# Hybrid decoder layer on one core: the order of short-convolution rows, the steps of the output projection's residuals, and the tile order of its last step

## The chip, the cores and the metric

One core of one Trainium2 chip. The metric is the device time of one execution in microseconds; the kernel before took 1410.79 us (median of 3 runs, 1409.48 to 1411.41).

## What is computed

One layer of a decoder step: 1104 rows of 1024 values (16 meta tokens, 1024 of a prompt, 64 of eight samples of eight). Cut to what matters here:

```python
hn = rmsnorm(h, norm_mix_pre)
proj = hn @ w_in                       # gate_b, gate_c, hv (512 each), z, xbc, dt
u = gate_c * hv
conv_u, _ = causal_dwconv(u, buf_sc, sconv_w)              # 3 taps
ya = group_rmsnorm(gate_b * conv_u, sconv_norm, 8)         # short convolution
...                                                        # SSD mixer gives yb (1024 wide)
mix = concatenate([ya, yb], -1) @ w_out
h = h + rmsnorm(mix, norm_mix_post)
f = rmsnorm(h, norm_ffn_pre)
y = h + rmsnorm((silu(f @ w_gate) * (f @ w_up)) @ w_down, norm_ffn_post)
```

All of it is float32; each product is made of matmuls of high and low parts (`hi`/`lo`, `...h`/`...l` in the names), two or three for one.

## The kernel before

The input is normalised and transposed (to 45 us), then projected row by row (a row is 128 channels for all tokens, in three pieces of 272, 320 and 512 columns, `CUTS`). Up to about 400 us PE (TensorE) does the SSD mixer's rows; the `z` rows and the short convolution's rows are the filling, which a generator hands out. The short convolution has four groups of 128 channels, j = 0 to 3, and three kinds of row for each, in the order of the string `SORD` (L43): `c` is the gate (`pc`, copied to `gc` by ACT), `v` the values (`ph`; DVE multiplies them by the gate, L649, and then the three taps follow, ACT L249 and DVE L252, written over `gc`), `b` the output (`pb`; L662 multiplies by `gc`, then squares, a matmul `sn` for the group sums, square root, reciprocal L672, product L673, and the store of the row to `d_ya`, L674, on SP's queue). The pieces of a row take turns in two PSUM buffers (`acc`, `NACC` = 2): the third piece waits until the first has been read.

Then the output projection, L985 to L1027: the token tiles go in three groups, (1,2,3), (4,9,5) and (6,7,8), with twelve steps n = 0 to 11 each, one for every 128 rows of `w_out` (k = 4 to 11, then 0 to 3). A step loads a piece of weights (`wo`), splits it (`woh` by ACT L998, `wol` by DVE L999) and does the matmuls L1007 of the group's tiles one after the other into two banks each. The mixing tiles come from DRAM (`mrb`, `mra`, L947) and are split into `mhb`/`mlb` and `mha`/`mla` (L954, L98). A finished group's tiles are copied (`h_tile`, L887 on ACT and L888 on DVE) and kept in `pend`. In the steps of the group after, `residual` is called for them at the steps of the list `RES`, and `fn_tile` at the steps of `FNS`. `residual` is a square sum on ACT (`ms`, L147), mean on DVE (L139), power on POOL (L141), and L899 and L900 on DVE; `fn_tile` another square sum (`hs`), power, L916 on DVE, eight transposes on PE (`fT`, L928) and copies to `xr` and `B1` (L931 or L933). For the last group both are called behind the loop, around `first(0)`, the first product of the FFN.

The FFN's gate and up products go by seven products for each block; `first(q)` (L1062) does four half products on PE: gate, up, gate, up (`xg`, `xu`; L1048). After a first half ACT copies it (`p1g`, `p1u`, L1077); the second half adds to the same PSUM, so it waits for that copy. The PSUM of `xg` is that of the last group's third tile in the list. Behind it come sums on DVE (L1189 to L1202: `T2`, `T3`, `T1`, `B22`; L1041: `s2g` and others) for the next products, `yg` and `zg`. The down projection ends the kernel.

The program's order is not the order on the engines: the scheduler of the framework takes an instruction by its priority and by a model of when it could start. `tc.high_priority(offset=...)` puts an instruction forward by so many places. So a change of a list can move rows on every engine.

## Time and profile before

| | us |
|---|---|
| median of 3 runs | 1410.79 |
| the profiled execution | 1407.59 |
| its span, first to last instruction | 1405.9 |
| PE busy | 1371.6 |
| DVE busy | 973.9 |
| ACT busy | 586.6 |
| mean granted clock of PE | 0.997 |

The profile is of one execution. A row of the timeline has its start, its length, engine, line, operation, output from inputs, shape, and in brackets how long the engine was idle before it and what ended that. DVE is VectorE, ACT ScalarE, POOL GpSimd, SP the queue that issues the DMAs. Where a release is named, it is the last one that the profile saw.

### The profile page before, as it was taken

The numbers are of one execution on the slowest core, as the hardware profiler recorded it, in microseconds if no ns is written. First come the engines' busy times: TensorE is split into PE (matmuls) and PEld (weight loads), VectorE is DVE, ScalarE is ACT, GpSimd is POOL, SyncE is SP. The second block draws the span as 40 slices with busy tenths as digits, with TensorE's granted clock in tenths as the row PEclk, the third lists the DMA queues.
The fourth block names the chain that finished last, engine by engine and source line by source line (L and its number), as shares of the span: only waits on it lengthen the run. The fifth ranks groups of instructions, "written<-read, shape, count | busy, mean of one in ns | idle before, by whom it ended". The sixth has DMA issues, their size and how long they took to land.

```text
span 1405.9 us, 22011 instructions
## 1 busy us (share of the span) xinstructions
PE 1371.6 (98%) x8841; PEld 1229.4 (87%) x8841; DVE 973.9 (69%) x1334; ACT 586.6 (42%) x947; POOL 50.0 (4%) x106
## 2 busy tenths in 40 slices
PE   7999999999999998999999999999999999999997
PEld 5889998878888986887889999999999998888886
DVE  6655457877888987687489877666767666455565
ACT  6465345434354344566554232222332234343431
POOL 1000000000000100011000000000000000000001
PEclk9999999999999999999999999999999999999999
DMA  6135347667736447765445553445333469655554
GB/s 213 47 103 153 94 125 197 204 175 204 216 116 209 130 133 273 249 225 179 149 137 181 183 203 115 161 165 175 133 131 113 163 222 323 226 178 168 168 166 139
DMA packets 212543, 240.51 MB, mean 171 GB/s; under 512 B 33421, under 2 KB 161505, under 8 KB 212442
## 3 DMA queue, kind: packets, MB, share of 16 engines
q1 hardware_dynamic: 212442, 239.12, 53.4%
q8 instruction: 69, 1.13, 0.3%
q14 instruction: 32, 0.26, 0.1%
HBM read 170.29 MB, written 68.79 MB: 170 GB/s over the span
## 4 chain that ended last, share of the span: by engine, by line
PE 84%; DVE 6%; DMA 5%; ACT 2%; issue 1%; SPq 1%; POOL 0%; DVEq 0%; POOLq 0%; ACTq 0%
PE d L1391 15%; PE px L220 10%; PE o L1007 9%; PE yg L1048 7%; PE yu L1048 7%; PE zg L1048 4%; PE zu L1048 4%; PE pz L220 4%; PE xg L1048 4%; PE xu L1048 4%; PE pc L220 3%; PE pb L220 3%; DMA M<-d_a 2%; PE ph L220 2%; PE pd L572 1%
## 5 line engine op out<-in xcount | busy, mean ns | idle before, releaser
L220 PE MATMUL px<-xh,whi 128*128 128x272 f32 (+2 forms) x288 | 94.8, 337 | 0.0
L220 PE MATMUL px<-xl,whi 128*128 128x272 f32 (+2 forms) x288 | 93.7, 333 | 0.0
L220 PE MATMUL px<-xh,wlo 128*128 128x272 f32 (+2 forms) x288 | 93.4, 332 | 0.0
L98 DVE TENSOR_TENSOR wlo<-raw,whi 128x1024 fp32r<-128x1024 f32 x32 | 39.1, 1220 | 44.8 <-ACT whi L106 43.5
L999 DVE SCALAR_TENSOR_TENSOR wol<-wo,vec,woh 128x1024 fp32r<-128x1024 f32 x36 | 46.0, 1278 | 31.5 <-ACT woh L998 31.5
L220 PE MATMUL pz<-xh,whi 128*128 128x256 f32 (+2 forms) x192 | 64.8, 337 | 0.2 <-DVE z L627 0.2
L220 PE MATMUL pz<-xh,wlo 128*128 128x256 f32 (+2 forms) x192 | 63.9, 333 | 0.0
L220 PE MATMUL pz<-xl,whi 128*128 128x256 f32 (+2 forms) x192 | 63.8, 332 | 0.0
L998 ACT ACTIVATE woh<-wo,vec 128x1024 fp32r<-128x1024 f32 x36 | 41.4, 1150 | 49.7 <-PE o L1007 44.1
L220 PEld LDWEIGHTS px<-xh,whi 128*128 128x128 f32 x288 | 54.5, 192 | 4.2
L220 PEld LDWEIGHTS px<-xl,whi 128*128 128x128 f32 x288 | 54.0, 190 | 4.2 <-issue 0.2
L220 PEld LDWEIGHTS px<-xh,wlo 128*128 128x128 f32 x288 | 54.0, 191 | 3.7
L1391 PE MATMUL d<-wd,B01h 128*128 128x512 f32 x176 | 54.2, 389 | 0.0
L252 DVE SCALAR_TENSOR_TENSOR xa<-xr,vec,xa 128x1128 f32<-128x1128 f32 x36 | 50.1, 1391 | 1.2 <-ACT xa L249 0.5
L1391 PE MATMUL d<-wd,T3h 128*128 128x512 f32 x152 | 46.8, 389 | 0.0
L1007 PE MATMUL o<-wol,mhb 128*128 128x512 f32 x144 | 44.3, 393 | 1.4 <-DVE wol L999 1.4
L1391 PE MATMUL d<-wd,B11h 128*128 128x512 f32 x144 | 44.2, 389 | 0.0
L1391 PE MATMUL d<-wd,T2h 128*128 128x512 f32 x144 | 44.2, 389 | 0.0
L556 ACT ACTIVATE M<-M,a_tok 128x128 f32<-128x128 f32 (+1 forms) x72 | 21.7, 383 | 47.8 <-DMA M<-d_a 37.9
L279 ACT ACTIVATE xr<-px 128x272 f32<-128x272 f32 (+2 forms) x36 | 16.3, 456 | 60.0 <-PE px L220 60.0
L1007 PE MATMUL o<-woh,mhb 128*128 128x512 f32 x144 | 39.5, 397 | 1.9 <-DVE gc L662 0.8
L1007 PE MATMUL o<-woh,mlb 128*128 128x512 f32 x128 | 40.0, 390 | 0.0
(691 smaller groups left out, 4094.5 us busy)
## 6 DMA issues: line engine op xcount, KB each, us to landing
wo<-in_w_out_dram SPq DMA_DIRECT2D x36, 512.0 KB, 3.5
raw<-in_w_in_dram SPq DMA_DIRECT2D x32, 512.0 KB, 6.0
wg<-in_w_gate_dram SPq DMA_DIRECT2D x11, 1024.0 KB, 8.4
wu<-in_w_up_dram SPq DMA_DIRECT2D x11, 1024.0 KB, 5.1
xr<-in_w_down_dram SPq DMA_DIRECT2D x11, 1024.0 KB, 5.3
d_t<-xr SPq DMA_DIRECT2D x11, 1024.0 KB
xt<-in_x_prompt_dram SPq DMA_DIRECT2D x16, 512.0 KB, 6.4
M<-d_a SPq DMA_DIRECT2D x16, 512.0 KB, 5.9
```

Source lines behind the costliest of these rows:

```text
L98: V.tensor_tensor(out=out, in0=a, in1=hi.bitcast(F32), op=ALU.subtract)
L220: PE.matmul(acc, (hi, lo, hi)[q][:, wk], (xh, xh, xl)[q][t][:, k, o:], start=n_ == 0, stop=n_ + 1 == len(order))
L252: V.scalar_tensor_tensor(out=dst, in0=part(row, i), scalar=wv[:, wcol(i):wcol(i) + 1], in1=dst, op0=ALU.mult, op1=ALU.add)
L279: S.activation(row[:, rc], pt[:, pc], AF.Copy)
L556: S.activation(M[:w, h, :w], M[:w, h, :w], AF.Relu, scale=-1.0, bias=a_s)
L572: PE.matmul(pdv[64 * e:64 * e + 64, h // 2, :w], xd[:w, h * 64:(h + 1) * 64], Ms[h // 8][:w, h % 8, :w], start=True, stop=True)
L998: S.activation(hi, raw, AF.Copy, scale=nv)
L999: V.scalar_tensor_tensor(out=lo, in0=raw, scalar=nv, in1=hi[:, :].bitcast(F32), op0=ALU.mult, op1=ALU.subtract)
L1007: PE.matmul(accs[i][c], l[:, kb, :], r_[:, c * 512:(c + 1) * 512], start=n == 0 and q == 0, stop=n == 11 and q == len(steps) - 1)
L1048: PE.matmul(acc[:, c, 0:W1], w_[l][k], b[r_][:, k, c * W1:(c + 1) * W1], start=start and k == 0 and x == 0, stop=k == 3 and x == 2, skip_g ...
L1391: PE.matmul(accs[t], sx[x][:, tl], wx[y], start=st and x + y == 0, stop=en and x == 1, skip_group_check=n not in OPENS)
```

## The change

Four edits. `SORD` has `v3` before `b2` instead of after it. `RES` and `FNS`, the steps at which a finished group's residuals and norm tiles are issued, go from 1, 2, 3 and 5, 6, 7 to 1, 3, 5 and 4, 6, 8. In the last group's last step the list of tiles is turned, so that tile 8's matmuls stand first, and since `pend` is made from the same list, its copies, residual and norm tile come first too (8, 6, 7). The copy by DVE instead of ACT in `fn_tile` goes from tile 8 to tile 7, which is now the last.

```diff
-SORD = "c0 c1 v0 v1 b0 c2 b1 v2 c3 b2 v3 b3"
-RES = [1, 2, 3]
-FNS = [5, 6, 7]
+SORD = "c0 c1 v0 v1 b0 c2 b1 v2 c3 v3 b2 b3"
+RES = [1, 3, 5]
+FNS = [4, 6, 8]
...
-                if q == 1 and i == GROUPS[-1][-1]:
+                if q == 1 and i == GROUPS[-1][1]:
                     V.tensor_copy(xr[q][n][:, :, cs], pt[:, :, ts])
...
+            if n == 11 and gi + 1 == len(GROUPS):
+                tiles = tiles[2:] + tiles[:2]
             for i in tiles:
```

Lines from L1001 on have numbers higher by 2 in the changed kernel.

DVE at the end of the short convolution, before. `gc_4220` is group 2's row and `gc_4618` group 3's, `pb` the pieces of a `b` row:

```order
425 L999 SCALAR_TENSOR_TENSOR wol_5202<-wo_5199,vec,woh_5201 128x1024
426 L673 TENSOR_TENSOR gc_4220<-gc_4220,sq_4849 128x512
427 L252 SCALAR_TENSOR_TENSOR gc_4618<-u_4921,vec,gc_4618 128x1024
428 L252 SCALAR_TENSOR_TENSOR gc_4618<-u_4921,vec,gc_4618 128x64
429 L588 TENSOR_TENSOR yf_5418<-yf_5418,zt_5420 128x1024
430 L252 SCALAR_TENSOR_TENSOR gc_4618<-u_4921,vec,gc_4618 128x1024
431 L252 SCALAR_TENSOR_TENSOR gc_4618<-u_4921,vec,gc_4618 128x64
432 L593 TENSOR_TENSOR zt_5420<-zt_5420 128x2x256
433 L662 TENSOR_TENSOR gc_4618<-pb_0_5022,gc_4618 128x256
434 L662 TENSOR_TENSOR gc_4618<-pb_1_5056,gc_4618 128x320
435 L98 TENSOR_TENSOR mlb_5180<-mrb_5177,mhb_5179 128x1024
```

The same place now, from the first read of group 3's `b` row on; its taps stand at 410 to 416, between the rows of group 2:

```order
424 L662 TENSOR_TENSOR gc_4220<-pb_2_4983,gc_4220 128x512
425 L673 TENSOR_TENSOR gc_4220<-gc_4220,sq_4944 128x256
426 L999 SCALAR_TENSOR_TENSOR wol_5202<-wo_5199,vec,woh_5201 128x1024
427 L672 RECIPROCAL sq_4944<-sq_4944 128x320
428 L662 TENSOR_TENSOR gc_4618<-pb_0_5022,gc_4618 128x256
429 L98 TENSOR_TENSOR mlb_5180<-mrb_5177,mhb_5179 128x1024
430 L98 TENSOR_TENSOR mlb_5186<-mrb_5183,mhb_5185 128x1024
431 L673 TENSOR_TENSOR gc_4220<-gc_4220,sq_4944 128x320
432 L588 TENSOR_TENSOR yf_5418<-yf_5418,zt_5420 128x1024
433 L672 RECIPROCAL sq_4944<-sq_4944 128x512
434 L662 TENSOR_TENSOR gc_4618<-pb_1_5056,gc_4618 128x320
```

The first read of group 3's `b` row (L662) no longer follows that group's taps directly; the first two mixing tiles' splits (L98) now stand between its first and second read.

SP's queue at the same place, before; `mrb` are the first mixing tiles, `fso` the final SSD state, `gc_4220` the short convolution's row 2:

```order
191 L579 DMA d_y_87<-y_4725 128x1024
192 L602 DMA d_yb_76<-yf_4801 128x1024
193 L584 DMA yf_5418<-d_y_87 128x1024
194 L586 DMA zt_5420<-d_z 128x8x128
195 L800 DMA out_dram<-fso 128x8x128
196 L995 DMA wo_5305<-in_w_out_dram 128x1024
197 L674 DMA d_ya<-gc_4220 128x1088
198 L947 DMA mrb_5177<-d_yb_70 128x1024
199 L947 DMA mrb_5183<-d_yb_71 128x1024
```

And now:

```order
191 L579 DMA d_y_87<-y_4725 128x1024
192 L800 DMA out_dram<-fso 128x8x128
193 L602 DMA d_yb_76<-yf_4801 128x1024
194 L947 DMA mrb_5177<-d_yb_70 128x1024
195 L947 DMA mrb_5183<-d_yb_71 128x1024
196 L586 DMA zt_5420<-d_z 128x8x128
197 L584 DMA yf_5418<-d_y_87 128x1024
198 L995 DMA wo_5305<-in_w_out_dram 128x1024
199 L947 DMA mrb_5189<-d_yb_72 128x1024
```

The loads of the first mixing tiles no longer stand behind the store of the short convolution's row 2.

ACT at the end of the output projection, before; `ms` and `hs` are the square sums of a tile's residual and of its norm tile, `p1g` the copy in the first FFN product:

```order
431 L887 ACTIVATE h_6433<-o_5990 128x512
432 L887 ACTIVATE h_6436<-o_5991 128x512
433 L147 ACTIVATE ms6j,ms_6447<-h_6433 128x1024
434 L887 ACTIVATE h_6439<-o_5992 128x512
435 L979 ACTIVATE weu1hi<-weu_6427 128x1024
436 L147 ACTIVATE ms7j,ms_6459<-h_6436 128x1024
437 L147 ACTIVATE ms8j,ms_6471<-h_6439 128x1024
438 L1077 ACTIVATE p1g_6507<-xg_6482 128x544
439 L147 ACTIVATE hs6j,hs_6591<-h_6433 128x1024
440 L1077 ACTIVATE p1u_6534<-xu_6509 128x544
441 L147 ACTIVATE hs7j,hs_6611<-h_6436 128x1024
```

And now:

```order
431 L887 ACTIVATE h_6433<-o_5992 128x512
432 L147 ACTIVATE ms8j,ms_6447<-h_6433 128x1024
433 L887 ACTIVATE h_6436<-o_5990 128x512
434 L979 ACTIVATE weu1hi<-weu_6427 128x1024
435 L887 ACTIVATE h_6439<-o_5991 128x512
436 L147 ACTIVATE ms6j,ms_6459<-h_6436 128x1024
437 L147 ACTIVATE ms7j,ms_6471<-h_6439 128x1024
438 L147 ACTIVATE hs8j,hs_6591<-h_6433 128x1024
439 L147 ACTIVATE hs6j,hs_6611<-h_6436 128x1024
440 L1079 ACTIVATE p1g_6507<-xg_6482 128x544
441 L147 ACTIVATE hs7j,hs_6631<-h_6439 128x1024
```

Tile 8's copy and square sum have moved to the front, and two square sums of norm tiles, `hs8` and `hs6`, instead of none now stand ahead of `p1g`.

## The prediction

> **What bounds the kernel now.** I read the page first: the share of each engine, and the chain that ended last.

> ```profile
> span 1405.9 us, 22011 instructions
> PE 1371.6 (98%) x8841; PEld 1229.4 (87%) x8841; DVE 973.9 (69%) x1334; ACT 586.6 (42%) x947; POOL 50.0 (4%) x106
> PE 84%; DVE 6%; DMA 5%; ACT 2%; issue 1%; SPq 1%; POOL 0%; DVEq 0%; POOLq 0%; ACTq 0%
> ```

> PE (TensorE) is busy 1371.6 of 1405.9 us, and the change takes no matmul away and adds none. So it can gain only what PE waits, in the places that it reorders, and lose only by new waits. The profiled execution took 1407.59 us (its span and 1.7 around it), 3.2 under the median of 1410.79; differences worked out on the profile are put on the median unchanged. 0.2%, 2.8 us, is about what a measurement of this kernel can tell from no change.

> Next I read PE's waits, in a window from 400 to 560 us (end of the short convolution, first steps of the output projection) and one from 560 to 770 (rest of it, first FFN products). Columns: who waits, for whom, total us, times, longest.

> ```profile
> PE pb L220 <- DVE gc L662: 3.6, 1, 3.6
> PE o L1007 <- DVE gc L662: 0.8, 1, 0.8
> PE o L1007 <- ACT woh L998: 0.8, 1, 0.8
> ```
> ```profile
> PE yg L1048 <- DVE u3g L1113: 1.4, 1, 1.4
> PE o L1007 <- DVE wol L999: 1.4, 1, 1.4
> PE fT L928 <- ACT xr L933: 1.4, 2, 0.7
> PE xg L1048 <- ACT h L887: 1.3, 1, 1.3
> PE xg L1048 <- ACT p1g L1077: 0.7, 1, 0.7
> PE yg L1048 <- DVE s2g L1041: 0.6, 1, 0.6
> ```

> That is 5.2 us around 530 to 550, 1.4 at the change of tile groups near 650, and 5.4 from 695 to 760. These three places are all that the change can touch. The largest wait also slows what follows. The timeline of PE shows it (start, us, what, idle before it):

> ```profile
> 529.22 0.31 PE L220 MATMUL pb<-xl,whi 128*128 128x320 f32 x1
> 533.14 0.80 PE L220 MATMUL pb<-xh,whi 128*128 128x512 f32 x1 [3.61 <-DVE gc L662]
> 533.73 0.63 PE L220 MATMUL pb<-xh,wlo 128*128 128x512 f32 x1
> 536.23 0.40 PE L220 MATMUL pb<-xh,wlo 128*128 128x512 f32 x1
> 536.46 0.40 PE L220 MATMUL pb<-xl,whi 128*128 128x512 f32 x1
> ```

> From 533.14 to 536.23 seven matmuls start, 3.09 us; at the later spacing of 0.23 they would take 1.63. So the idle time of 3.61 costs 1.46 more: 5.07 in all.

> **The first edit: v3 before b2.** The third piece of b3 needs the PSUM buffer that b3's first piece leaves when DVE's L662 has read it. That read stood behind v3's taps:

> ```profile
> 528.14 1.48 DVE L252 SCALAR_TENSOR_TENSOR gc<-u,vec,gc 128x1024 f32<-128x1024 f32 x2 [0.92 <-ACT gc L249]
> 532.66 0.82 DVE L662 TENSOR_TENSOR gc<-pb,gc 128x256 f32<-128x256 f32 x2
> ```

> The row of 529.22 is the end of b3's second piece, so the first was over some 3.5 us before it; its read came at 532.66. Afterwards PE does v3 where b2 was, and b2 (48 projection matmuls of its last two pieces among them) lies between v3 and b3. So the taps fall on b2's time, and the read of b3's first piece has only a reciprocal ahead of it: I work it out at 527.1, from the order and these durations, some 4 us before PE needs the buffer at 531 (its matmuls up to there, without the waits), since three output-projection matmuls and `sn30` now lie between too. The 3.61 and the 1.46 should go. The two waits of 0.8 come from the same backlog on DVE and ACT; I take them as gone, and hold open that both stay. Gain: 3.61 + 1.46 + 0.82 + 0.84 = 6.7, from 4.5 (something of the wait is left) to 6.9.

> One thing is new: output-projection matmuls now stand on PE in front of b3's third piece, so PE needs the first mixing tiles (`mrb` loaded by SP, split into `mhb` and `mlb`) at 529.5 instead of 545. Before, their loads were issued late, behind the store of b2's row on SP:

> ```profile
> 529.54 9.89 SPq L947 DMA_DIRECT2D mrb<-d_yb x4
> ```
> ```profile
> L954 ACT ACTIVATE mhb<-mrb x9: 614/1061/1066, 535.6 to 624.8; 128x1024 fp32r<-128x1024 f32 x8, 128x512 fp32r<-128x512 f32 x1
> ...
> DMA to landing us min/median/max: 3.3/4.7/6.0
> ```

> Afterwards they stand ahead of that store, behind `fso`'s store and `d_yb`'s, which I work out at 519.5 to 520. With 6.0 us to land and one ACT pass each, `mhb` is there at 527.2, 2 us before it is needed. That margin is an estimate; it makes a rival.

> **The second edit: residuals at steps 1, 3, 5.** At 650 the low part of a weight row waited behind two residual operations on DVE, and PE waited for it:

> ```profile
> 650.13 1.27 DVE L899 SCALAR_TENSOR_TENSOR h<-h,mr5r,post_bc 128x1024 f32<-128x1024 f32 x1
> 651.32 1.27 DVE L999 SCALAR_TENSOR_TENSOR wol<-wo,vec,woh 128x1024 fp32r<-128x1024 f32 x1
> ```

> With the third residual two steps later, L999 starts at 650.13: 1.19 of PE's 1.44 goes. The other moved residuals and norm tiles lie under matmuls of steps where PE has no wait. Between 0.5 and 1.4, I take 1.2.

> **The third and fourth edits: tile 8 first in the last step.** The first FFN product `xg` needs the banks of tile 8. It waited 1.30 for their copies; now they are free 2 us earlier, and it starts at 696.79 - 1.30 = 695.5. But the list of tiles also gives the order of the residuals, and on ACT the copy `p1g`, which the second half of `xg` waits for, now comes after `hs8` and `hs6` (the order in the section on the change). Before, it stood ahead of `hs6`:

> ```profile
> 700.11 0.62 ACT L1077 ACTIVATE p1g<-xg 128x544 f32<-128x544 f32 x1 [0.20 <-PE xg L1048]
> 700.98 1.06 ACT L147 ACTIVATE hs6j<-h 128x1024 bf16<-128x1024 f32 x1 [0.24 <-DVE mr L139]
> ```

> `hs6` needs tile 6's finished residual, and that is a row of DVE work in order. Durations:

> ```profile
> 694.35 0.69 DVE L888 COPY h<-o 128x512 f32<-128x512 f32 x1 [0.58 <-ACT h L887]
> 697.33 1.28 DVE L899 SCALAR_TENSOR_TENSOR h<-h,mr6r,post_bc 128x1024 f32<-128x1024 f32 x1 [0.72 <-POOL mr6r L141]
> 698.53 1.22 DVE L980 TENSOR_TENSOR weu1lo<-weu,weu1hi 128x1024 fp32r<-128x1024 f32 x1
> 699.66 1.22 DVE L900 TENSOR_TENSOR h<-h,xt 128x1024 f32<-128x1024 f32 x1
> ```
> ```profile
> 696.75 0.55 POOL L141 TENSOR_TENSOR mr6r<-mr,mhalf 128x1 f32<-128x1 f32 x1 [37.19 <-DVE mr L139]
> ```

> `ms8` ends at 695.6 (its last matmul at 693.5, a copy, 1.06 for itself), POOL's power by 696.7, L899 of tile 8 starts at 696.8. From one start to the next these rows take 1.20, 1.13 and 1.14, a copy 0.6. L899 of tile 8, `weu1lo`, tile 7's copy, L900 of tile 8: 1.20 + 1.13 + 0.6 + 1.14 gives 700.9. Then tile 6's power, 0.8 until L899 starts at 701.8; L899 of tiles 6 and 7, 2.4; L900 of tile 6, done at 705.5. `hs6` 1.06, `p1g` 0.62: 707.2. PE has two first halves to do from 695.5; by the row of `p1g` the first took from 696.79 to 700.0, 3.1 to 3.2, so PE is through at 701.7 and waits 5.5 us, with the slow stretch after it (1.46 by the row above) 7.0.

> [...]

> What goes here: 1.30 of `xg` and 2 x 0.69 of `fT`, whose results are ready by then. The second product's `xg` starts at 695.5 + 15.1 (its 16.5 before, from 696.79 to the row below, less 1.38 idle) + 7.0 = 717.6, 4.3 later:

> ```profile
> 713.31 0.50 PE L1048 MATMUL xg<-B01h,weg1hi 128*128 128x272 f32 x2
> 714.22 2.43 DVE L1192 TENSOR_TENSOR xr<-xr,xr 128x2176 f32<-128x2176 f32 x1 [1.44 <-ACT xr L933]
> 736.38 0.68 DVE L1041 TENSOR_TENSOR s2g<-sg,s2g 128x512 fp32r<-128x512 f32 x1
> 741.20 2.42 DVE L1189 TENSOR_TENSOR T1l<-xr,T1h 128x2176 fp32r<-128x2176 f32 x1
> 744.16 2.42 DVE L1189 TENSOR_TENSOR B22l<-xr,B22h 128x2176 fp32r<-128x2176 f32 x1
> ```

> `T1l` and `B22l` stood behind `s2g`. DVE's row from L1192 on starts 2.1 later (it waits for tile 8's copies, whose residual now comes first), and has `T1l` and `B22l` (2 x 2.33) ahead of `s2g`: ready at 743.8. PE came to `s2g` at 736.5 (736.38 + 0.74, less the wait of 0.62); now 4.3 later, less the 0.71, and with some 2.1 of the third product's matmuls moved ahead of it, at 742.2: 1.6 idle. The waits of 0.71 and 1.44 are covered by that delay. So here 5.45 goes (1.30 + 1.38 + 0.71 + 0.62 + 1.44) and 5.5 + 1.46 + 1.6 = 8.6 comes: 3.1 lost, from 0.5 (each step of the chain a little shorter, no slow stretch) to 5 (POOL's powers beside DVE, and 0.71 and 1.44 kept).

> **Sum.** -6.7 - 1.2 + 3.1 = -4.8: 1402.8 on the profiled execution, **1406.0** on the median. By the bounds above, from -7.8 to 0, that is 1403 to 1410.8.

> **Rivals.** *A: no wait at `p1g`.* If DVE's chain is done some 5 us sooner, or the wait is covered, the last step brings only its gains: -6.7 - 1.2 - 2.7 = -10.6, 1400.2. For it: ACT has few operations here. Against it: the order on ACT is fixed, and DVE's chain rests on measured durations.

> *B: the gain at the short convolution moves elsewhere.* The windows show DVE's room (the third number after the length of the stretch is DVE's busy time; the numbers after POOL's are PE's clock, DMA share and GB/s):

> ```profile
> 480.00:520.00 40.00, 40.00 (x267) 33.81 (x267) 34.99 (x39) 16.39 (x32) 4.52 (x1) 1.00 0.46 146
> 520.00:560.00 40.00, 34.73 (x170) 28.39 (x169) 32.70 (x39) 16.52 (x20) 1.32 (x2) 0.96 0.71 242
> ```

> It is idle 12.3 us of these 80, and its work stays the same while PE's time shrinks by 6.7. If 3 to 4 us of it come back as waits for `sn31`, `sn32` or a weight row, -6.7 becomes -3 and the sum -1, 1409.8: no change.

> *C, slower: PE waits for `mhb`.* If SP gets to the `mrb` loads no sooner than before, `mhb` is there at 536.7 (529.54, 6.0 to land, 1.1 on ACT), and PE, which needs it at 529.5, waits 7.2 and then runs slow for 1.46. The first edit then loses 8.7 - 6.7 = 2.0 instead of gaining, and the sum is +2.0 - 1.2 + 3.1 = +3.9: 1414.7. It decides once `mhb` is later than some 533, the loads issued after 526. For it: DVE's `mlb` waits in the same place, so a late load also stops DVE. Against it: nothing on SP ahead of the loads waits for b2 or v3 any more.

> That the change does nothing can be left out: the orders on ACT, DVE and SP are others.

> **Numbers.** The forecast 0.55, A 0.13, B 0.16, C 0.16. Of the forecast's 0.55 some 0.05 lies within 2.8 us of no change, of B 0.13, with 0.02 faster and 0.01 slower. So faster 0.50 + 0.13 + 0.02 = 0.65; same 0.05 + 0.13 = 0.18; slower 0.16 + 0.01 = 0.17. The range takes in A and B and leaves out most of C: 1400 to 1412.

> **What would show it.** Right: no wait of `pb` for `gc`, `mrb` issued before 521, L999 at 650 ahead of L899 of tile 5, a wait of `xg` for `p1g` of 4 to 6 us near 707 with slow matmuls behind it, and `s2g` at about 743. Wrong: `o` waiting for `mhb` near 530 (C); new waits of `o` or `sn` from 535 to 550 (B); `p1g` at its place near 700 (A).

## The result, and the profile after

The changed kernel took 1404.25 us (median of 6 runs, 1402.11 to 1405.63) against 1411.1 beside it: a ratio of 0.9947 with a 95% interval of 0.9932 to 0.9963, 7.5 us less (5.2 to 9.6). In a second set of runs, told below, it was 0.9967 (0.9950 to 0.9984). The forecast was 4.8 us less. The profiled execution took 1402.11.

Page of the changed kernel, its span, its engines and the chain that ended last:

```profile
span 1400.4 us, 22011 instructions
PE 1369.7 (98%) x8841; PEld 1230.6 (88%) x8841; DVE 973.9 (70%) x1334; ACT 586.2 (42%) x947; POOL 51.8 (4%) x106
PE 90%; DVE 3%; DMA 3%; ACT 2%; issue 1%; SPq 1%; POOL 0%; DVEq 0%; POOLq 0%; ACTq 0%
```

DVE's share of the chain fell from 6% to 3%, and that of DMA from 5% to 3%. PE's waits after, in the same two windows (400 to 560 us, then from 560 on):

```profile
PE pb L220 <- DVE u L649: 0.5, 1, 0.5
```
```profile
PE xg L1050 <- ACT p1g L1079: 5.7, 1, 5.7
PE yg L1050 <- DVE s2g L1043: 2.6, 1, 2.6
PE o L1009 <- DVE h L888: 0.2, 1, 0.2
PE o L1009 <- DVE wol L999: 0.2, 1, 0.2
PE yu L1050 <- ACT s2u L1042: 0.2, 1, 0.2
```

Of the nine waits that the prediction listed, eight are gone or down to 0.2; that for `s2g` has grown, and a large new one has come for the first product's `p1g`. (The 0.5 us for `u` was there before, too.) Where the time went can be read by taking the same rows in both traces. The row `po` at 499.34 before (498.18 after), ahead of every wait that the change removes, starts 1.16 us sooner after; that is a difference of two executions and belongs to no edit. At the row of 641.22 before (632.55 after) it is 8.67 sooner, so the short convolution and the first group gave 7.5. At the weight row of 652.65 (642.78) it is 9.87: 1.2 more. At the end, 1405.9 and 1400.4, it is 5.5: from the last step on 4.4 were lost.

First place, DVE and SP of the changed kernel at the end of the short convolution:

```profile
525.41 0.36 DVE L662 TENSOR_TENSOR gc<-pb,gc 128x256 f32<-128x256 f32 x1
525.69 2.35 DVE L98 TENSOR_TENSOR mlb<-mrb,mhb 128x1024 fp32r<-128x1024 f32 x2
```
```profile
517.64 1.61 SPq L947 DMA_DIRECT2D mrb<-d_yb  x2
```
```profile
522.91 2.00 ACT L954 ACTIVATE mhb<-mrb 128x1024 fp32r<-128x1024 f32 x2
```
```profile
528.26 0.63 PE L1009 MATMUL o<-woh,mhb 128*128 128x512 f32 x2
```

The first read of `b3` starts 7.2 us sooner than before (1.2 of it is the execution's), and PE runs through. The loads of the mixing tiles were issued at 517.6, not 529.5, their split is over by 524.9, and PE uses them at 528.3.

Last place, ACT and PE of the changed kernel behind the output projection:

```profile
691.62 1.06 ACT L147 ACTIVATE hs8j<-h 128x1024 bf16<-128x1024 f32 x1
...
696.04 1.06 ACT L147 ACTIVATE hs6j<-h 128x1024 bf16<-128x1024 f32 x1 [3.27 <-DVE h L900]
...
697.09 0.60 ACT L1079 ACTIVATE p1g<-xg 128x544 f32<-128x544 f32 x1
```
```profile
691.65 0.41 PE L1050 MATMUL xu<-B01h,weul 128*128 128x272 f32 x2
697.75 0.82 PE L1050 MATMUL xg<-B11h,wegh 128*128 128x272 f32 x2 [5.69 <-ACT p1g L1079]
698.37 0.66 PE L1050 MATMUL xg<-B11l,wegh 128*128 128x272 f32 x2
...
732.11 0.41 PE L1050 MATMUL yg<-T2l,s2g 128*128 128x272 f32 x2
735.14 1.27 PE L1050 MATMUL yg<-T2h,s2g 128*128 128x272 f32 x4 [2.61 <-DVE s2g L1043]
```

`hs6` waits 3.27 us for L900, `p1g` stands behind it with its input long there, and PE with it. The windows give the clock behind both waits (third number from the right):

```profile
697.00:701.40 4.40, 3.65 (x19) 3.65 (x20) 3.83 (x6) 2.48 (x7) 1.10 (x2) 0.61 1.02 338
734.00:739.00 5.00, 3.86 (x20) 3.86 (x20) 5.00 (x9) 0.24 (x1) 0.00 (x0) 0.66 0.63 246
```

0.61 over 4.4 us and 0.66 over 5 are 1.7 us of clock lost each. By the starts of the matmuls it is 1.4 to 1.5: 16 of them start from 735.14 to 738.61, in 3.47 us, where the later spacing of two in 0.25 would take 2.0.

### The profile page after: what moved, and what is told of

It reads as the page before. It is cut to its first block, busy times and chain, and to the rows that moved or that the text cites. A ratio compares the mean times of both kernels' runs of the same rounds, so it can differ in the third digit from the quotient of the medians.

```text
span 1400.4 us, 22011 instructions
## 1 busy us (share of the span) xinstructions
PE 1369.7 (98%) x8841; PEld 1230.6 (88%) x8841; DVE 973.9 (70%) x1334; ACT 586.2 (42%) x947; POOL 51.8 (4%) x106
## 3 DMA queue, kind: packets, MB, share of 16 engines
q8 instruction: 69, 1.13, 0.3%
## 4 chain that ended last, share of the span: by engine, by line
PE 90%; DVE 3%; DMA 3%; ACT 2%; issue 1%; SPq 1%; POOL 0%; DVEq 0%; POOLq 0%; ACTq 0%
PE d L1393 15%; PE px L220 10%; PE o L1009 9%; PE yu L1050 7%; PE yg L1050 7%; PE pz L220 5%; PE zu L1050 5%; PE zg L1050 5%; PE xg L1050 5%; PE xu L1050 5%; PE pb L220 3%; PE pc L220 3%; PE ph L220 2%; DMA M<-d_a 1%; PE pd L572 1%
## 5 line engine op out<-in xcount | busy, mean ns | idle before, releaser
L220 PE MATMUL px<-xh,whi 128*128 128x272 f32 (+2 forms) x288 | 94.6, 336 | 0.1
L220 PE MATMUL px<-xl,whi 128*128 128x272 f32 (+2 forms) x288 | 93.7, 333 | 0.0
L220 PE MATMUL px<-xh,wlo 128*128 128x272 f32 (+2 forms) x288 | 93.3, 332 | 0.0
L98 DVE TENSOR_TENSOR wlo<-raw,whi 128x1024 fp32r<-128x1024 f32 x32 | 39.0, 1220 | 45.5 <-ACT whi L106 45.4
L999 DVE SCALAR_TENSOR_TENSOR wol<-wo,vec,woh 128x1024 fp32r<-128x1024 f32 x36 | 46.0, 1278 | 32.2 <-ACT woh L998 32.1
L220 PE MATMUL pz<-xh,whi 128*128 128x256 f32 (+2 forms) x192 | 64.6, 337 | 0.0
L220 PE MATMUL pz<-xh,wlo 128*128 128x256 f32 (+2 forms) x192 | 63.9, 333 | 0.0
L220 PE MATMUL pz<-xl,whi 128*128 128x256 f32 (+2 forms) x192 | 63.7, 332 | 0.0
L998 ACT ACTIVATE woh<-wo,vec 128x1024 fp32r<-128x1024 f32 x36 | 41.4, 1149 | 49.1 <-PE o L1009 45.9
L220 PEld LDWEIGHTS px<-xh,whi 128*128 128x128 f32 x288 | 54.4, 192 | 4.6 <-ACT xr L279 0.3
L220 PEld LDWEIGHTS px<-xl,whi 128*128 128x128 f32 x288 | 53.9, 190 | 4.2 <-issue 0.2
L220 PEld LDWEIGHTS px<-xh,wlo 128*128 128x128 f32 x288 | 54.0, 190 | 3.7
L252 DVE SCALAR_TENSOR_TENSOR xa<-xr,vec,xa 128x1128 f32<-128x1128 f32 x36 | 50.1, 1391 | 1.2 <-ACT xa L249 0.5
L220 PEld LDWEIGHTS pz<-xh,whi 128*128 128x128 f32 x192 | 36.1, 188 | 3.9 <-issue 1.3
```

The costliest lines, as they stand in the source:

```text
L98: V.tensor_tensor(out=out, in0=a, in1=hi.bitcast(F32), op=ALU.subtract)
L220: PE.matmul(acc, (hi, lo, hi)[q][:, wk], (xh, xh, xl)[q][t][:, k, o:], start=n_ == 0, stop=n_ + 1 == len(order))
L252: V.scalar_tensor_tensor(out=dst, in0=part(row, i), scalar=wv[:, wcol(i):wcol(i) + 1], in1=dst, op0=ALU.mult, op1=ALU.add)
L998: S.activation(hi, raw, AF.Copy, scale=nv)
L999: V.scalar_tensor_tensor(out=lo, in0=raw, scalar=nv, in1=hi[:, :].bitcast(F32), op0=ALU.mult, op1=ALU.subtract)
```

## The experiments

The theory: the places add up. The first edit gives 7.5 us, the second 1.2, and the last step's two edits take 4.4 back, by ACT's order at `p1g`. The first edit, the second, and the last step's two together were each run alone; then the last step was mended in three ways. The fourth edit, the copy by DVE for tile 7 instead of tile 8, was never run by itself.

**The first edit alone.**

```diff
-SORD = "c0 c1 v0 v1 b0 c2 b1 v2 c3 b2 v3 b3"
+SORD = "c0 c1 v0 v1 b0 c2 b1 v2 c3 v3 b2 b3"
```

> Only the first edit: v3 ahead of b2. Theory (the places add up, each as the two profiles show it): PE's waits of 3.6, 0.8 and 0.8 us go and the half clock behind the first with them, and the rows after read 7.5 us sooner, so about 7.5 us under before, 1403.6, with the wait of 1.4 for wol near 650 and the waits of 1.3, 1.4, 0.7, 0.6 and 1.4 from 695 to 760 still there. Rival (the waits at the short convolution come back elsewhere when the residuals stay at steps 1, 2, 3): a gain of 3 us or less, with new waits of o in the first steps.

1401.49 us against 1409.99, ratio 0.9940 (0.9925 to 0.9954): 8.5 less (6.5 to 10.6). Its trace has none of the waits for `gc` and `woh`; that of 1.4 for `wol` and all those from 695 to 760 stand as before. The gain is the first edit's, and none of it is lost again later.

**The second edit alone.**

```diff
-RES = [1, 2, 3]
-FNS = [5, 6, 7]
+RES = [1, 3, 5]
+FNS = [4, 6, 8]
```

> Only the second edit: residuals at steps 1, 3, 5 and norm tiles at 4, 6, 8. Theory: the wait for wol near 650 falls from 1.44 to 0.2 us, everything else stays: 1.2 us under before, 1409.9. Rival (a moved residual or norm tile stands in the way of some other step): no change or up to 2 us slower, with a new wait of o of 1 us or more between 560 and 690.

1409.07 against 1409.99, ratio 0.9998 (0.9988 to 1.0008). The wait itself did what was expected; PE's row at that place:

```profile
654.70 0.73 PE L1007 MATMUL o<-wol,mhb 128*128 128x512 f32 x2 [0.22 <-DVE wol L999]
```

It has no new wait from 560 to 690, against the rival. (At 460 us, in the short convolution, it has one of 1.1 us of `ph` for `gc` that before has not. Of the two executions of the first two edits told below, one has it too, with 0.8, and one has not, so it varies with the execution.) But the time cannot be told from no change: 1.2 us is inside the interval (1.7 less to 1.1 more). The mechanism is shown, its worth in time is not.

**The last step's edits alone.** As in the diff of the change, with `SORD`, `RES` and `FNS` as before.

> Only the third and fourth edits: tile 8 first in the last step. Theory: the last step alone makes the kernel slower; xg starts 1.3 us sooner, but PE waits 5.7 us for p1g, 2.6 us for s2g, and each of the two is followed by half a clock: 4.4 us over before by the difference of the two profiles from 650 on, 1415.5. Rival (DVE sets the time from 715 to 770 anyway, so that the wait for p1g is paid back): no change, 1411.

1415.2 against 1409.99, ratio 1.0034 (1.0022 to 1.0047): 4.8 slower (3.1 to 6.6). PE's waits from 560 to 800 of that kernel:

```profile
PE xg L1050 <- ACT p1g L1079: 5.7, 1, 5.7
PE yg L1050 <- DVE s2g L1043: 2.7, 1, 2.7
PE o L1009 <- DVE wol L999: 1.4, 1, 1.4
```

One more, of 0.2, is left out. So the loss is real and DVE pays nothing back. The three runs of edits alone sum to -8.5 - 0.3 + 4.8 = -4.0, beside -7.5 and -4.7 for the whole in two sets; within their intervals they add.

**The first two edits without the last step's**, run in two sets.

> The first two edits without the last step's. Theory: 7.5 and 1.2 us, 8.7 under before, 1402.4, some 2 to 4 us faster than the whole change; p1g in its old place, no wait for it. Rival (the last step costs nothing, or is needed for the rest): the time of the whole change, 1404 to 1405, or slower.

> The first two edits once more, beside the two kernels of this call on one chip: 1400 us, 9 to 10 under before.

1400.05 against 1409.99, ratio 0.9929 (0.9916 to 0.9942), and 1401.37 against 1411.63, 0.9935 (0.9922 to 0.9948). Not the 1404 or more of the rival, and faster than the whole change by its second set (0.9950 to 0.9984); with its first (0.9932 to 0.9963) the intervals overlap.

**The whole change, beside two mended last steps.**

> The whole change once more, beside the two kernels of this call on one chip: 1404 us, 7 under before, with the waits of 5.7 us for p1g and 2.6 for s2g.

1405.49 against 1411.26, ratio 0.9967. The same waits. But the clock behind that of 5.7 us was halved for two stretches instead of one: the windows of this execution,

```profile
697.95:701.37 3.42, 1.95 (x8) 1.95 (x9) 2.85 (x5) 2.97 (x6) 1.17 (x3) 0.50 0.87 307
701.37:704.78 3.41, 3.41 (x18) 3.41 (x17) 1.85 (x2) 1.59 (x2) 0.00 (x0) 0.50 0.52 154
704.78:708.19 3.41, 3.41 (x30) 3.41 (x30) 0.00 (x0) 1.99 (x4) 0.00 (x0) 1.00 0.00 0
```

and those of the first profile of the same program:

```profile
697.25:700.66 3.41, 2.91 (x13) 2.91 (x14) 2.84 (x5) 2.00 (x4) 1.10 (x2) 0.50 1.01 332
700.66:704.07 3.41, 3.41 (x30) 3.41 (x29) 0.89 (x1) 2.87 (x4) 0.00 (x0) 1.00 0.25 75
```

That is 1.7 us of clock between two executions of one program. Of the four profiles with this wait, the first has one stretch; this one, that of the last step's edits alone and that of `s2g` first below have two (in the last two, the rows of two matmuls start 0.45 us apart from 708.74 to 710.56 and from 699.95 to 703.97, and 0.25 apart from 711.68 and 704.28 on). It may be why the two sets differ, but most executions have no trace, so this is not shown.

**The copies first.** A one-element copy that reads `p1g` stands ahead of `hs8`, one that reads `p1u` ahead of `hs6`, so ACT's order is fixed by data:

```diff
+        if behind is not None:
+            S.activation(junk[:w, 0:1], behind[:w, 0, 0:1], AF.Copy)
         S.activation(junk[:w, :], src, AF.Square, accum_out=ss[:w])
...
-        r = rstd_of(square_sum(ph, h[:w, :], w, f"hs{i}"), w, DM, f"hr{i}")
+        r = rstd_of(square_sum(ph, h[:w, :], w, f"hs{i}", p1s.get({8: ("g", 0), 6: ("u", 0)}.get(i))), w, DM, f"hr{i}")
```

> The whole change, with the copies p1g and p1u of the first product put ahead of the square sums hs8 and hs6 on ACT by a one-element copy that reads them. Theory (the wait comes from ACT's order alone): the wait of 5.7 us for p1g and the half clock behind it (1.7 us) go; DVE has s2g ahead of T1l and B22l again, so its 2.6 us and 1.7 us go in good part. Between 6 and 11 us under the whole change, 1394 to 1398. Rival (DVE's chain of residuals is what bounds, and the wait only moves to the transposes fT, to L1194's inputs and to s2g): 0 to 3 us under the whole change, with waits of fT or yg of 4 us or more in their place.

1401.37, 4.1 under the whole change beside it (ratio to before 0.9933, 0.9910 to 0.9956). That is less than the theory's 6 to 11 and more than the rival's 0 to 3; but the interval overlaps a little with that of the whole change (0.9950 to 0.9984), so the time alone decides for neither. PE's waits from 560 to 800:

```profile
PE fT L931 <- DVE hr L139: 3.0, 1, 3.0
PE yg L1053 <- DVE u3g L1117: 1.4, 1, 1.4
PE xg L1053 <- ACT p1g L1081: 0.7, 1, 0.7
```

Two more, of 0.2 each, are left out. The wait of 5.7 is gone, and that for `s2g` with it (DVE has `s2g` ahead of `T1l` again). In their place the transposes of tile 8, which now stand in the middle of the last half product, wait 3.0 for the norm tile, and half a clock follows from 701.0 to 704.4 (rows of two matmuls 0.45 us apart until 704.28, 0.25 from 704.60 on). The source of that wait on DVE:

```profile
696.61 2.35 DVE L902 TENSOR_TENSOR h<-h,xt 128x1024 f32<-128x1024 f32 x2
698.88 0.15 DVE L139 TENSOR_SCALAR hr<-hs 128x1 f32<-128x1 f32 x1
699.75 1.29 DVE L919 SCALAR_TENSOR_TENSOR hn<-h,hr8r,ffn_bc 128x1024 f32<-128x1024 f32 x1 [0.73 <-POOL hr8r L141]
```

So both are true: ACT's order made the 5.7, and DVE's chain of residuals, with tile 8's norm tile behind it, was next.

**`s2g` first.** `T1` and `B22` are split behind the weights of the g sums; the rest is the whole change:

```diff
-    bsplit(T1, b11, p1s["u", 2])
-    bsplit(B22, b22, p1s["u", 2])
+    bsplit(T1, b11, ws0["g"][4][0][0][:, None, 0:1].bitcast(F32))
+    bsplit(B22, b22, ws0["g"][4][0][0][:, None, 0:1].bitcast(F32))
```

> The whole change with the wait for p1g kept, and only the splits of T1 and B22 put behind the weights of the g sums, so that s2g stands ahead of T1l and B22l on DVE as before the change. Theory (the place of T1l and B22l costs the 2.6 us): s2g is there 4.7 us sooner, its wait and the half clock behind it go, and the time falls by 2 to 4 us, 1400 to 1402; less if zg then waits for T1l. Rival (the wait for s2g is only the debt of the late start at 707, so whatever stands first waits): no change, with zg waiting for T1l or B22l instead.

1404.25, 1.2 under the whole change beside it, ratios 0.9956 (0.9942 to 0.9970) and 0.9967: not told apart. PE's waits:

```profile
PE xg L1050 <- ACT p1g L1079: 5.7, 1, 5.7
PE yg L1050 <- DVE u3g L1115: 1.4, 1, 1.4
PE yu L1050 <- ACT s2u L1042: 1.0, 1, 1.0
PE zg L1050 <- DVE T1l L1191: 0.3, 1, 0.3
```

The wait of 2.6 is gone, as the place of `T1l` and `B22l` would have it, and 2.7 us of others stand there instead: DVE's rows are late as a whole, as the rival said, though `zg`, which it named, waits only 0.3. No half clock follows these waits (from 726 to 746 the rows of two matmuls start 0.25 us apart), which is 1.7 us less than in the whole change, about what the medians differ by.

**Matmuls in the new order, residuals in the old.**

```diff
-                if q == 1 and i == GROUPS[-1][1]:
+                if q == 1 and i == GROUPS[-1][-1]:
...
-        pend = [(i, h_tile(i, accs[i])) for i in tiles]
+        pend = sorted(((i, h_tile(i, accs[i])) for i in tiles), key=lambda e: GROUPS[gi].index(e[0]))
```

The copy by DVE is back at tile 8, which is the last again.

> The whole change, but only the matmuls and copies of the last step go 8, 6, 7; residuals and norm tiles go 6, 7, 8 as before. Theory (the order of the residuals did the harm, since hs6 stands ahead of p1g behind tile 8's work on DVE): hs6 is done at about 701.9 of the time of before instead of 706.7, so the wait of xg for p1g falls from 5.7 to 1 us with no half clock behind it, s2g stands ahead of T1l again; 4 to 6 us under the whole change, 1400 to 1402. And no better than the first two edits alone, because DVE's chain to L1194 and s2g does not get shorter when PE starts 1.3 us sooner: the waits of fT grow by what the wait of xg loses. Rival (the sooner start of xg is worth its 1.3 us): 1398.5, more than 1 us under the first two edits.

1401.9 against 1401.37 for the first two edits beside it, ratios 0.9933 (0.9917 to 0.9949) and 0.9935. The wait for `p1g` falls to 2.08 (1 was expected), and half a clock no longer follows (the rows of two matmuls behind it, from 696.63 on, start 0.25 us apart); the sooner start of `xg` is worth nothing that can be measured:

```profile
696.28 0.52 PE L1050 MATMUL xg<-B11h,wegh 128*128 128x272 f32 x2 [2.08 <-ACT p1g L1079]
700.39 0.52 PE L1050 MATMUL xu<-B11h,weuh 128*128 128x272 f32 x2 [0.85 <-ACT p1u L1079]
```

So the price of the last step lay in the order of the residuals and norm tiles, not in that of the matmuls. Where the 1.3 went was expected of `fT`; it went to `p1g` and `p1u`, while `fT` waits no more.

**Means on POOL**, with the first two edits alone:

```diff
-        V.tensor_scalar(out=v[:w], in0=ss[:w], scalar1=1.0 / d, scalar2=EPS, op0=ALU.mult, op1=ALU.add)
+        (E or V).tensor_scalar(out=v[:w], in0=ss[:w], scalar1=1.0 / d, scalar2=EPS, op0=ALU.mult, op1=ALU.add)
```

with E = POOL for `hr6`, `hr7` and `hr8`.

> The first two edits, and the means of the last group's norm tiles (three one-column operations between hs and the power) on POOL instead of DVE, so that they no longer stand behind the residuals of the next tiles there. Theory (DVE's chain of residuals bounds the stretch from 695 to 740): hn6 stands ahead of the two additions L900, the two waits of 0.7 for fT fall, L1192 starts up to 1 us sooner; 0.5 to 2 us under the first two edits, 1398 to 1399.5. Rival (the stretch is set by ACT's order, hs7 and hs8 behind the table load and f): no change or 1 us slower.

1401.28, ratio 0.9930 (0.9914 to 0.9947): the first two edits' time. The waits of `fT` fell from 1.4 to 1.1 in all. So the theory failed: the small operations on DVE are not what this stretch hangs on.

## Why the prediction was right, and where its terms were off

*The first edit, -6.7.* The mechanism was right in each step: the read of `b3`'s first piece was worked out at 527.1 and came at 525.4 (1.2 of that is the execution's sooner start), the loads at 519.5 to 520 and came at 517.6, `mhb` at 527.2 and came by 524.9, and all three waits went together. The size was somewhat low: measured were 7.5 on the profile and 8.5 (6.5 to 10.6) alone; in the profile of the edit alone, from the row `po` to the first `xg`, 197.45 became 190.64, 6.8. The 0.7 between the two profiles is in no wait that they list. Rival B, new waits in the first steps, did not come, and C, PE waiting for `mhb`, had 3.4 us to spare.

*The second edit, -1.2.* The wait of 1.44 became 0.22. As time, 1.2 us is less than these runs can tell from nothing.

*The last step, +3.1.* The wait for `p1g` was forecast at 5.5 and was 5.69, with ACT's order as its cause; the last step alone (5.7 again) and the copies first (none) show it. The waits for `fT`, for `h`, for the second product's `p1g` and for `u3g` went, as said. The mis-sized term is the wait for `s2g`: 1.6 was forecast without a slow stretch, it was 2.61 with one, 2.5 us more. Put on the clock of this execution (9.87 sooner by the weight row above), the forecast has PE at `s2g` at 732.3 and `s2g` ready at 733.9. PE came at 732.5, but `s2g` was ready at 735.1, 1.2 later. DVE's row from L1194 on began 0.6 later than forecast, and before `s2g` DVE waited longer for the load of `wu`, 0.55 before the change and 1.24 after:

```profile
735.77 0.69 DVE L1089 TENSOR_TENSOR wu<-wu 128x512 f32<-128x512 f32 x1 [0.55 <-DMA wu<-in_w_up_dram]
```
```profile
707.01 2.42 DVE L1194 TENSOR_TENSOR xr<-xr,xr 128x2176 f32<-128x2176 f32 x1 [5.46 <-ACT xr L933]
727.92 0.69 DVE L1091 TENSOR_TENSOR wu<-wu 128x512 f32<-128x512 f32 x1 [1.24 <-DMA wu<-in_w_up_dram]
734.40 0.68 DVE L1043 TENSOR_TENSOR s2g<-sg,s2g 128x512 fp32r<-128x512 f32 x1
```

That a wait of that length costs only itself, with no slow stretch behind it, rested on no row: the trace of before had, after 400 us, waits up to 1.44 and one of 3.61, and none between. The stretch behind `p1g` was forecast as one (1.46), which holds in this execution and not in the three with two. The loss was 4.4 on the profile and 4.8 (3.1 to 6.6) alone, against 3.1. By its terms it would be 5.9 (5.69 + 2.61 + 0.17 of waits and 1.4 + 1.5 of slow stretches, less the 5.45 gone); the 1.5 between is not found in any row.

*The sum, -4.8.* The profiles give -7.5 - 1.2 + 4.4 = -4.3, the first set of runs -7.5 (5.2 to 9.6) and the second -4.7. So 4.8 lies outside the interval of the first set and inside that of the second. That the sum came so near is in part luck: the gain of the first edit was put too low by 0.8 on the profile (1.8 by its run alone) and the loss of the last step too low by 1.3 (1.7), and the two errors cancel. The windows show 1.7 us of clock lost behind the wait of 3.61 before the change (0.50 from 532.72 to 536.13) and as much behind that of 2.61 in the changed kernel (0.50 from 734.79 to 738.20), where the starts of the matmuls gave 1.46 and 1.5.

Rival A, no wait at `p1g`, did not come by itself, but the kernel without that wait (the copies first) and the one with a shorter wait and no slow stretch (matmuls only) gained no more than the first two edits. What A left out is that DVE's chain is next behind ACT's order; its -10.6 was never to be had.

## What to carry to other kernels

A list that sets the order of matmuls may also set the order of what follows on other engines: look at who reads it last. Before an order is moved, look on each engine at what now stands ahead of the operation that the bottleneck waits for; here one square sum ahead of one 0.6 us copy cost as much as half the gain. And judge the parts of a change one by one: here the first did all the good that could be measured, and the last step's part, left out, left a faster kernel than the whole.

## What was not expected of the hardware

A wait of PE of 2.20 us was followed by half a clock in one execution, and one of 2.87 was not in another. Both are at the same place of the SSD part; the rows show the wait and the clock behind it, first the last step's edits alone (the clock falls from 1.00 to 0.50):

```profile
301.30 1.48 PE L750 MATMUL s0p<-ident,s 128*128 128x128 f32 x8 [2.20 <-DVE s L766]
298.44:301.85 3.41, 1.21 (x11) 1.00 (x10) 3.31 (x7) 3.41 (x8) 0.00 (x0) 1.00 0.00 0
301.85:305.27 3.42, 3.42 (x16) 3.42 (x15) 3.42 (x5) 2.40 (x4) 0.00 (x0) 0.50 0.95 281
```

and the whole change (the clock stays at 1.00):

```profile
302.31 1.09 PE L750 MATMUL s0p<-ident,s 128*128 128x128 f32 x8 [2.87 <-DVE s L766]
297.88:301.30 3.42, 1.56 (x14) 1.36 (x12) 3.31 (x11) 3.05 (x10) 0.00 (x0) 1.00 0.00 0
301.30:304.71 3.41, 2.40 (x19) 2.40 (x20) 3.41 (x4) 2.94 (x4) 0.00 (x0) 1.00 0.47 129
```

Nor did half a clock follow the 2.08 of the kernel with matmuls only, or any wait of 1.44 us or less in the traces of before and of the changed kernel from 400 us on. So the waits of 2 to 3 us had a price that differed by 1.7 us from one execution to another, and one of 5.7 was followed by one such stretch or by two.
